# Keeping scaled attention tiles in PSUM and issuing a projection piece between a step's scores and its transposes

## The chip, the cores and the metric

The kernel runs on one core of one Trainium2 chip. The core's engines work side by side, each through its own queue in order: TensorE (PE, with PEld for its weight loads), VectorE (DVE), ScalarE (ACT), GpSimd (POOL) and SyncE (SP, which here only starts transfers). The metric is the device time of one execution in microseconds. The runs of the kernel before took 1247.38, 1249.82 and 1250.08 us; their median, 1249.82 us, is the time to compare with.

## The reference

A two-layer encoder trunk over 512 positions and 1024 channels, in fp32. Layer 0 is a state-space mixer and a gated MLP; layer 1 is a differential attention and a gated MLP. The change lies in the attention alone:

```python
qkv = h @ w_qkv                                   # 8 heads, each with 2 q and 2 k of 64, one v of 128
q = q * (64 ** -0.5)
s = einsum('bqhtd,bkhtd->bhtqk', qi, k) + bias    # t = 0, 1
p = softmax(s)
pd = p[:, :, 0] - lam * p[:, :, 1]
out = einsum('bhqk,bkhe->bqhe', pd, v)
out = rmsnorm(out, subln_g) * (1.0 - lambda_init)
return out @ w_o
```

## The kernel before

Every matrix product is made of three fp32r matmuls (`mm3`): a value is held as a high part `hi` and a low part `lo` = value - `hi`, and hi by hi, hi by lo and lo by hi are added up in one PSUM bank. So each tile that feeds a product is first written as its high part by ACT, then as its low part by DVE, which needs the value and the high part. Weights are split in the same way: ACT writes the high part (line 139), and in the attention POOL writes the low part (line 141).

The attention is a hand-written order of 32 steps, four 128-row query blocks `q` for each of eight heads `hd`. PSUM has eight banks, given out by tag: `sc` 3, `tr` 1, `pj` 2, `pv` 1, `aux` 1. A step `i` issues:

- `scores(i)`: four matmuls (lines 1207 and 1210) into two `sc` banks, then on DVE two fused add-and-maximum operations (line 1214) and the negated maxima (line 1217).
- `lower()`: the low parts of a q or k projection that was scaled a step earlier (line 1141, two operations).
- `transp(i - 2)`: four transposes (line 1242) of the finished probabilities of step i - 2, ACT's copy to the high part (1244) and DVE's low part (1245). In a late step (i = 6, 10, 14, ...) `pv` comes here instead, the twelve matmuls of a finished head with v, and the transposes follow it.
- `expo(i)` (ACT, 1222), `norm2(i - 1)` (DVE, 1232: writes the probabilities that the next step transposes).
- `flush()`, which runs what waits in the list `post`: the scaling of a finished projection (`evac`), and the low part of a head's output.
- `fl()`, twice (once from step 25 on): a piece of other work, in `fill`. Up to step 24 it is a quarter of a q or k projection of a later head: two blocks of `mm3`, six matmuls (lines 778 to 780) into a `pj` bank. From step 25 on it is an output projection of heads 0 to 3, `ofull`, also into a `pj` bank.
- in some steps the head's RMS norm: `sub1` (row sums, and Newton steps on POOL), `sub2` (broadcast), and at the start of the next step `sub3`.

`evac` scales a projection's bank into an SBUF tile `tq` (line 1133); ACT copies `tq` to the high parts (1137) and, a step later, `lower()` subtracts (1141). `sub3` does the same for a head's output: line 1270 from the `pv` bank into `tq`, 1274 and 1275 for the two parts. Both `tq` come from tag `sqt`, which has two buffers.

The first head's two projections run ahead of the loop, each flushed, and `lower()` follows; then `fl(6)` issues six pieces, the first of which opens head 1's q projection.

Of the kernel before, what the change touches and what calls it, by code (L numbers as in the profile page):

```python
# [9 lines left out]
F32 = mybir.dt.float32  # L10
# [27 lines left out]
def trunk(ctx, tc, xs, xt, sp, bx, cx, sv, vec, lamv, biasw, wglu, wup, wdn, wv, wqk, wo, out):  # L38
# [3 lines left out]
    def pool(name, bufs, side=None, space=None):  # L42
        kw = dict(name=name, bufs=bufs, reuse_waits="tile")
        if side:
            kw["side"] = side
        if space:
            kw["space"] = space
        return tc.alloc_tile_pool(**kw)
# [7 lines left out]
    def arena(dt, shape, name):  # L56
        return ap_.tile(shape, dt, tag="A", name=name)
# [553 lines left out]
    def intra(bk):  # L611
        yp = ps2.tile([128, 4, 8, 16], F32, tag="yp", name="yp", bufs=6)
        yb[bk] = yp
        for pl in range(4):
            for e in range(2):
                gi = (bk * 4 + pl) * 2 + e
                PE.matmul(yp[64 * e:64 * e + 64, pl], lhsT=u[:, gi], rhs=TT[:, :, gi], start=(pl == 0), stop=False,
                          skip_group_check=True)
# [5 lines left out]
    def out_half(bk, half, dr):  # L624

        yp = yb[bk]
        j0 = 32 * half
        for pl in range(4):
            pr = bk * 4 + pl
            for e in range(2):  # L630
                gl = (pr % 8) * 2 + e
                r0 = 64 * e + j0
                PE.matmul(yp[r0:r0 + 32, pl], lhsT=IZ[:, j0:j0 + 32, dr, e, pr], rhs=W[pr // 8][:, dr, gl],
                          start=False, stop=True, skip_group_check=True, tile_position=(0, r0))
# [21 lines left out]
    for at_s, kind, bk in EV:  # L656
        f = {"w": wchunk, "i": lambda bk=bk: intra(bk), "y": lambda bk=bk: S.copy(ys[:, bk - NB], yb.pop(bk)), "f": lambda bk=bk: out_half(bk, 0, 0),
             "b": lambda bk=bk: out_half(bk, 1, 1)}[kind]
# [112 lines left out]
    wk = pool("wk", 1, "left")  # L771
# [5 lines left out]
    def mm3(ps, wh, wl, xh, xl, first, last):  # L777
        PE.matmul(ps, lhsT=wh, rhs=xh, start=first, stop=False)  # L778
        PE.matmul(ps, lhsT=wh, rhs=xl, start=False, stop=False)  # L779
        PE.matmul(ps, lhsT=wl, rhs=xh, start=False, stop=last)  # L780
# [75 lines left out]
    for un in range(4):  # L856
# [3 lines left out]
        for ml in range(2):  # L860
# [4 lines left out]
            ps = psd[0].tile([128, 512], F32, tag="mm", name="ps", bufs=6)  # L865
# [206 lines left out]
    def bank(tag, name):  # L1072
        return psd[0].tile([128, 512], F32, tag=tag, name=name, bufs={"sc": 3, "tr": 1, "pj": 2, "pv": 1, "aux": 1}[tag])
# [29 lines left out]
    post = []  # L1103
# [5 lines left out]
    def lower():  # L1109
        for f in lows:  # L1110
            f()
        lows.clear()

    def flush():
        for f in post:
            f()
        post[:] = hold
        hold.clear()

    def proj(hd, which):  # L1120

        st = {}

        def evac(ps):
            if which == 0:  # L1130
                qk[hd] = at.tile([128, 5, 512], F32R, tag="qk", name="qkt", bufs=2)
            tq = wk.tile([128, 512], F32, tag="sqt", name="tq", bufs=2)
            V.scalar_tensor_tensor(tq, ps, 0.125 if which == 0 else 1.0, rbt, op0=ALU.mult, op1=ALU.mult)
            t = qk[hd]
            rows = (slice(0, 64), slice(64, 128))
            for c in range(2):
                S.activation(t[rows[c], 2 * which + c], tq[rows[c]], AF.Copy)

            def low():
                for c in range(2):  # L1140
                    V.tensor_tensor(t[rows[1 - c], c] if which == 0 else t[rows[c], 4], tq[rows[c]],  # L1141
                                    t[rows[c], 2 * which + c].bitcast(F32), op=ALU.subtract)

            lows.append(low)
            if which == 1:
                for c in range(2):
                    G.dma_start(out=t[rows[1 - c], 2 + c], in_=t[rows[c], 2 + c])

        def part(k0):
            def f():  # L1150
                if k0 == 0:
                    st["w"] = ws.start()
                    st["ps"] = bank("pj", "pj")
                if k0 % 4 == 0:
                    ws.split(k0 // 4, eng=G)
                wh, wl = st["w"]
                for k in range(k0, k0 + 2):
                    mm3(st["ps"], wh[:, k * 128:k * 128 + 128], wl[:, k * 128:k * 128 + 128], xhi[:, k], xlo[:, k],
                        k == 0, k == 7)
                if k0 == 6:  # L1160
                    post.append(lambda: evac(st["ps"]))
            return f
        return [part(k0) for k0 in (0, 2, 4, 6)]
# [33 lines left out]
    def load_bias(hd):  # L1197
        biases[hd] = at.tile([128, 896], F32, tag="bias", name="bias", bufs=2)
        SY.dma_start(out=biases[hd], in_=biasw[hd])

    def scores(i):
        hd, q = divmod(i, 4)
        t = qk[hd]
        mx = mxs[i] = at.tile([128, 8], F32, tag="mx", name="mx", bufs=4)
        pss = [bank("sc", "sc") for _ in range(2)]
        for c in range(2):
            PE.matmul(pss[c], lhsT=t[:, c, 128 * q:128 * q + 128], rhs=t[:, 2 + c], start=True, stop=False)
        for c in range(2):
            r = slice(64 * c, 64 * c + 64)
            PE.matmul(pss[c], lhsT=t[r, c, 128 * q:128 * q + 128], rhs=t[r, 4], start=False, stop=True)  # L1210
        sc[i] = []
        for c in range(2):
            s = at.tile([128, 512], F32, tag=f"s{c}", name="s", bufs=3 - c)
            V.tensor_tensor_reduce(s, pss[c], biases[hd][:, 384 - 128 * q:896 - 128 * q], op0=ALU.add, op1=ALU.max,
                                   scale=1.0, scalar=-3.0e38, accum_out=mx[:, c:c + 1])
            sc[i].append(s)
        V.tensor_scalar(mx[:, 2:4], mx[:, 0:2], -1.0, None, op0=ALU.mult)

    def expo(i):
        mx = mxs[i]  # L1220
        for c in range(2):
            S.activation(sc[i][c], sc[i][c], AF.Exp, bias=mx[:, 2 + c:3 + c], accum_out=mx[:, 4 + c:5 + c])

    def norm1(i):
        mx = mxs[i]
        V.reciprocal(mx[:, 6:8], mx[:, 4:6])
        V.tensor_tensor(mx[:, 7:8], mx[:, 7:8], nlam, op=ALU.mult)
        S.activation(sc[i][1], sc[i][1], AF.Copy, scale=mx[:, 7:8])
# [8 lines left out]
    def transp(i):  # L1237
        pd = pds.pop(i)
        q = i % 4
        ps = bank("tr", "ptp").rearrange("p (k t) -> p k t", t=128)  # L1240
        for kt in range(4):
            PE.transpose(ps[:, kt], pd[:, 128 * kt:128 * kt + 128], ident)
        hi, lo = ptt[:, :, 0, 128 * q:128 * q + 128], ptt[:, :, 1, 128 * q:128 * q + 128]
        S.activation(hi, ps, AF.Copy)
        return lambda: V.tensor_tensor(lo, ps, hi.bitcast(F32), op=ALU.subtract)
# [16 lines left out]
    def sub2(hd):  # L1262
        ps, _, rt = pvs.pop(hd)
        rb = rstd_bcast(rt, 128)
        pvs[hd] = (ps, rb)

    def sub3(hd):
        ps, rb = pvs.pop(hd)
        tq = wk.tile([128, 512], F32, tag="sqt", name="tq", bufs=2)
        V.scalar_tensor_tensor(tq, ps, gsub, rb, op0=ALU.mult, op1=ALU.mult)  # L1270
        if hd % 4 == 0:
            ot[hd // 4] = arena(F32R, [128, 4, 2, 512], f"o{hd}")
        o = ot[hd // 4]
        S.activation(o[:, hd % 4, 0], tq, AF.Copy)
        post.insert(0, lambda: V.tensor_tensor(o[:, hd % 4, 1], tq, o[:, hd % 4, 0].bitcast(F32), op=ALU.subtract))
# [14 lines left out]
    def fl(n=1):  # L1290
        for _ in range(n):
            if fill:
                fill.pop()()

    fl(6)
    for i in range(32):
        hd, q = divmod(i, 4)
        if q == 0 and 0 < hd < 7:
            load_bias(hd + 1)
        if i >= 9 and q == 1:  # L1300
            sub3((i - 9) // 4)
        if i >= 1:
            norm1(i - 1)
        scores(i)
        lower()
        late = i >= 6 and i % 4 == 2
        lo = transp(i - 2) if i >= 2 and not late else None
        if late:
            pv((i - 6) // 4)
        expo(i)  # L1310
        if lo:
            lo()
        if i >= 1:
            norm2(i - 1)
        if late:
            transp(i - 2)()
        flush()
        if i < 25:
            fl()
        if i >= 8 and q == 0:  # L1320
            sub2((i - 8) // 4)
        fl()
        if late:
            sub1((i - 6) // 4)
# [163 lines left out]
```

## Time and profile before

| what | value |
|---|---|
| median of the runs | 1249.82 us (1247.38 to 1250.08) |
| profiled execution, its own time | 1246.88 us |
| its span, first to last instruction | 1245.1 us |
| PE busy over the span | 1175.8 us, 94% |
| DVE busy | 824.9 us, 66% |
| ACT busy | 581.6 us, 47% |
| POOL busy | 253.5 us, 20% |
| mean granted TensorE clock | 0.982 |

The profiled execution is about 3 us below the median. Its span leaves out 1.8 us of its own time. Step 0 of the attention begins near 651 us and step 31 near 823 us of the span.

### The profile page before, as it was taken

The page shows a single profiled execution, that of the slowest core. Times are in us where ns is not written, and L with a number is a line of the kernel's source. Part 1 is how long each engine was busy: PE and PEld are TensorE (multiplying, and loading weights), DVE is VectorE, ACT ScalarE, POOL GpSimd, SP SyncE. Part 2 cuts the span into 40 slices and gives each one's busy share as a digit, 9 for nine tenths or more (in the row PEclk, how much of TensorE's full clock was granted, in tenths as well). Part 3 has the DMA queues.
Part 4 walks back from the last instruction along what each step waited for, and adds up shares of the span by engine and source line. Part 5 has one row for each costly group of instructions (what it writes and reads, how often), then busy time and mean ns, then how long its engine had stood idle before and what let it go on. Part 6 is the DMA issues. An engine that isn't in the chain of part 4 may idle for free.

```text
span 1245.1 us, 16497 instructions
## 1 busy us (share of the span) xinstructions
PE 1175.8 (94%) x6338; PEld 930.0 (75%) x6338; DVE 824.9 (66%) x1650; ACT 581.6 (47%) x1001; POOL 253.5 (20%) x271
## 2 busy tenths in 40 slices
PE   3875899999999999999998999999999999999996
PEld 1663588888878888878876777678888878888786
DVE  7989866676752467754339899976767643566634
ACT  6864655444431244333337777755444422344431
POOL 3899434000000000011033444523000000000011
PEclk8997999999999999999999999999999999999998
DMA  5005322122233222132332323221222233122222
GB/s 219 2 2 136 135 75 102 68 102 84 75 117 115 68 102 101 58 106 77 99 123 82 90 74 87 88 73 67 98 71 99 81 117 125 68 92 78 93 94 68
DMA packets 23391, 112.32 MB, mean 90 GB/s; under 512 B 2704, under 2 KB 5392, under 8 KB 16144
## 3 DMA queue, kind: packets, MB, share of 16 engines
q1 hardware_dynamic: 21472, 108.64, 25.7%
q0 software_dynamic: 1280, 2.10, 0.9%
q8 instruction: 50, 0.82, 0.3%
q10 hardware_dynamic: 560, 0.52, 0.1%
q14 instruction: 29, 0.24, 0.1%
HBM read 102.86 MB, written 2.10 MB: 84 GB/s over the span
## 4 chain that ended last, share of the span: by engine, by line
PE 83%; DVE 14%; ACT 2%; issue 1%; DMA 0%; SPq 0%; DVEq 0%; ACTq 0%
PE ps L779 20%; PE ps L778 20%; PE ps L780 20%; DVE scn L678 2%; PE pj L778 2%; PE pj L780 2%; PE pj L779 2%; DVE St L683 1%; PE vps L1088 1%; DVE qkt L1141 1%; PE vps L1090 1%; PE vps L1089 1%; DVE acc L681 1%; PE po L779 1%; PE po L780 1%; PE po L778 1%
## 5 line engine op out<-in xcount | busy, mean ns | idle before, releaser
L778 PE MATMUL ps<-xhi,hi 128*128 128x512 f32 x672 | 266.9, 397 | 0.0
L779 PE MATMUL ps<-xlo,hi 128*128 128x512 f32 x672 | 265.7, 395 | 0.0
L780 PE MATMUL ps<-xhi,lo 128*128 128x512 f32 x672 | 264.1, 393 | 0.0
L139 ACT ACTIVATE hi<-raw 128x1024 fp32r<-128x1024 f32 (+2 forms) x216 | 184.1, 874 | 113.5 <-PE ps L779 85.8
L141 DVE TENSOR_TENSOR lo<-raw,hi 128x1024 fp32r<-128x1024 f32 (+3 forms) x178 | 188.3, 1077 | 43.5 <-ACT hi L139 41.8
L903 DVE TENSOR_TENSOR tpb<-ps,rb 128x512 f32<-128x512 f32 x88 | 60.8, 693 | 149.7 <-PE ps L780 144.5
L905 ACT ACTIVATE acc<-tpb,vect 128x512 f32<-128x512 f32 x88 | 71.6, 816 | 168.2 <-DVE tpb L903 168.2
L780 PEld LDWEIGHTS ps<-xhi,lo 128*128 128x128 f32 x672 | 126.1, 188 | 31.5
L778 PEld LDWEIGHTS ps<-xhi,hi 128*128 128x128 f32 x672 | 126.1, 188 | 30.6
L779 PEld LDWEIGHTS ps<-xlo,hi 128*128 128x128 f32 x672 | 126.2, 188 | 29.5
L779 PE MATMUL ps<-act,hi 128*128 128x512 f32 (+1 forms) x374 | 144.1, 385 | 0.2
L778 PE MATMUL ps<-act,hi 128*128 128x512 f32 (+1 forms) x374 | 142.8, 382 | 0.0
L780 PE MATMUL ps<-act,lo 128*128 128x512 f32 (+1 forms) x374 | 142.1, 380 | 0.0
L803 POOL COPY ssum<-sqt 128x512 f32<-128x512 f32 x4 | 2.5, 627 | 658.5 <-ACT sqt L800 658.5
L981 DVE TENSOR_TENSOR h<-ps,h 128x512 f32<-128x512 f32 x30 | 20.7, 690 | 107.5 <-PE ps L780 107.5
L141 POOL TENSOR_TENSOR lo<-raw,hi 128x512 fp32r<-128x512 f32 (+1 forms) x38 | 61.0, 1611 | 114.2 <-ACT hi L139 114.1
L778 PEld LDWEIGHTS ps<-act,hi 128*128 128x128 f32 x374 | 70.3, 188 | 15.8
L780 PEld LDWEIGHTS ps<-act,lo 128*128 128x128 f32 x374 | 70.2, 188 | 15.9 <-DVE lo L141 1.4
L779 PEld LDWEIGHTS ps<-act,hi 128*128 128x128 f32 x374 | 70.2, 188 | 15.3 <-DVE act L922 1.1
L911 DVE SCALAR_TENSOR_TENSOR acc<-tpb,vect,acc 128x512 f32<-128x512 f32 x88 | 66.2, 752 | 3.1
L910 DVE SCALAR_TENSOR_TENSOR acc<-tpb,vect,acc 128x512 f32<-128x512 f32 x88 | 65.5, 744 | 0.6 <-ACT acc L905 0.6
L921 ACT ACTIVATE act<-acc 128x512 fp32r<-128x512 f32 x44 | 27.9, 634 | 66.2 <-DVE acc L920 66.2
(260 smaller groups left out, 2035.7 us busy)
## 6 DMA issues: line engine op xcount, KB each, us to landing
raw<-wup SPq DMA_DIRECT2D x44, 1024.0 KB, 4.8
raw<-wdn SPq DMA_DIRECT2D x32, 704.0 KB, 4.0
raw<-wqk SPq DMA_DIRECT2D x16, 512.0 KB, 3.5
raw<-wglu SPq DMA_DIRECT2D x4, 1024.0 KB, 4.9
raw<-wv SPq DMA_DIRECT2D x8, 512.0 KB, 3.5
raw<-wo SPq DMA_DIRECT2D x4, 1024.0 KB, 4.8
bias<-biasw SPq DMA_DIRECT2D x8, 448.0 KB, 4.1
cxt<-cx SPq DMA_DIRECT2D x1, 2064.0 KB, 15.8
```

The lines of the kernel that those rows point to most:

```text
L139: S.activation(hi[:, h0:h1], self.raw[i][:, h0:h1], AF.Copy)
L141: eng.tensor_tensor(lo[:, h0:h1], self.raw[i][:, h0:h1], hi[:, h0:h1].bitcast(F32), op=ALU.subtract)
L678: V.tensor_tensor(prd[dr], cur[:, dr].unsqueeze(1).to_broadcast([128, 2, 2, 32]), cft[dr], op=ALU.mult)
L778: PE.matmul(ps, lhsT=wh, rhs=xh, start=first, stop=False)
L779: PE.matmul(ps, lhsT=wh, rhs=xl, start=False, stop=False)
L780: PE.matmul(ps, lhsT=wl, rhs=xh, start=False, stop=last)
L903: V.tensor_tensor(tb[:, 1:513], ps, state["rb"], op=ALU.mult)
L905: S.activation(acc, tb[:, 1:513], AF.Identity, bias=cb, scale=cw[1])
L910: V.scalar_tensor_tensor(acc, tb[:, 0:512], cw[0], acc, op0=ALU.mult, op1=ALU.add)
L911: V.scalar_tensor_tensor(acc, tb[:, 2:514], cw[2], acc, op0=ALU.mult, op1=ALU.add)
L921: S.activation(hi, a0, AF.Copy)
L981: V.tensor_tensor(h[:, m], ps, h[:, m], op=ALU.add)
```

## The change

Two things. First, `evac` and `sub3` no longer scale into an SBUF tile: they write the scaled values back to the PSUM bank that they read, and ACT's copy to the high part and DVE's low part read that bank. Second, in a step up to 24 the first of the two pieces is issued right behind `lower()`, ahead of the transposes or `pv`; the list `post` is taken before it and run where `flush()` stood.

```diff
@@ proj(): evac
             if which == 0:
                 qk[hd] = at.tile([128, 5, 512], F32R, tag="qk", name="qkt", bufs=2)
-            tq = wk.tile([128, 512], F32, tag="sqt", name="tq", bufs=2)
+
+            tq = ps
             V.scalar_tensor_tensor(tq, ps, 0.125 if which == 0 else 1.0, rbt, op0=ALU.mult, op1=ALU.mult)
@@ sub3()
         ps, rb = pvs.pop(hd)
-        tq = wk.tile([128, 512], F32, tag="sqt", name="tq", bufs=2)
+        tq = ps
         V.scalar_tensor_tensor(tq, ps, gsub, rb, op0=ALU.mult, op1=ALU.mult)
@@ the loop over steps
         scores(i)
         lower()
         late = i >= 6 and i % 4 == 2
+        todo = post[:]
+        post.clear()
+        if i < 25:
+            fl()
         lo = transp(i - 2) if i >= 2 and not late else None
         if late:
             pv((i - 6) // 4)
...
             norm2(i - 1)
         if late:
             transp(i - 2)()
-        flush()
-        if i < 25:
-            fl()
+        for f in todo:
+            f()
         if i >= 8 and q == 0:
             sub2((i - 8) // 4)
         fl()
```

## Rows read from the trace of the kernel before

**Rows 1.** Windows, steps 7 to 22: PE, PEld, DVE, ACT, POOL us; clock; DMA

```profile
688.00:776.00 88.00, 87.08 (x434) 66.28 (x434) 80.61 (x177) 68.82 (x144) 38.58 (x77) 1.00 0.31 87
```

**Rows 2.** Waits view of the attention: us in total, times, longest

```profile
PE ptp L1242 <- DVE s L1232: 4.7, 6, 2.9
```

**Rows 3.** Timeline, transposes that waited: start, us, engine, line, [idle before <- releaser]

```profile
660.99 0.66 PE L1242 MATMUL ptp<-ident,s 128*128 128x128 f32 x4 [0.82 <-DVE s L1232]
667.05 0.63 PE L1242 MATMUL ptp<-ident,s 128*128 128x128 f32 x4 [1.69 <-DVE mx L1226]
677.02 0.63 PE L1242 MATMUL ptp<-ident,s 128*128 128x128 f32 x4 [1.35 <-DVE mx L1226]
699.01 0.63 PE L1242 MATMUL ptp<-ident,s 128*128 128x128 f32 x4 [0.24 <-DVE s L1232]
...
789.66 0.52 PE L1242 MATMUL ptp<-ident,s 128*128 128x128 f32 x3 [2.92 <-DVE s L1232]
```

**Rows 4.** Views of tiles and lines, whole attention: ns min/median/max

```profile
L1141 DVE TENSOR_TENSOR qkt<-tq,qkt x32: 676/686/3161, 643.9 to 797.4; 64x512 fp32r<-64x512 f32 x32
...
L1245 DVE TENSOR_TENSOR pt<-ptp,pt x32: 678/691/693, 665.6 to 835.2; 128x512 fp32r<-128x512 f32 x32
...
L1217 DVE TENSOR_SCALAR mx<-mx x32: 168/170/1244, 653.8 to 825.1; 128x2 f32<-128x2 f32 x32
```

**Rows 5.** Timeline, a weight split on POOL and DVE's operation beside it

```profile
698.24 1.76 POOL L141 TENSOR_TENSOR lo<-raw,hi 128x512 fp32r<-128x512 f32 x1 [2.18 <-ACT hi L139]
...
698.78 0.74 DVE L1270 SCALAR_TENSOR_TENSOR tq<-pvp,gsub,rb 128x512 f32<-128x512 f32 x1
```

**Rows 6.** Timeline, start of head 1's q projection

```profile
642.92 0.39 PE L778 MATMUL pj<-xhi,hi 128*128 128x512 f32 x1
...
643.92 0.68 DVE L1141 TENSOR_TENSOR qkt<-tq,qkt 64x512 fp32r<-64x512 f32 x1
```

**Rows 7.** Timeline, step 1 from its first piece to the next scores

```profile
656.21 0.50 PE L778 MATMUL pj<-xhi,hi 128*128 128x512 f32 x1
656.31 0.69 DVE L1214 CUSTOM_DVE_ANT_0 s<-sc,bias 128x512 f32<-128x512 f32 x1 [0.43 <-PE sc L1210]
...
657.65 1.06 DVE L1217 TENSOR_SCALAR mx<-mx 128x2 f32<-128x2 f32 x1
...
658.75 1.40 DVE L1141 TENSOR_TENSOR qkt<-tq,qkt 64x512 fp32r<-64x512 f32 x2
...
659.12 0.62 PE L1207 MATMUL sc<-qkt 128*128 128x512 f32 x2
```

**Rows 8.** Timeline, the late step 10 (first two) and steps 11 and 12

```profile
702.62 0.68 DVE L1275 TENSOR_TENSOR o<-tq,o 128x512 fp32r<-128x512 f32 x1
...
703.28 0.50 PE L778 MATMUL pvp<-pt,v 128*128 128x512 f32 x1
...
713.37 0.74 DVE L1232 SCALAR_TENSOR_TENSOR s<-s,mx 128x512 f32<-128x512 f32 x1
...
714.54 0.20 POOL L162 TENSOR_TENSOR t<-t 128x4 f32<-128x4 f32 x1
...
715.62 0.69 DVE L1214 CUSTOM_DVE_ANT_0 s<-sc,bias 128x512 f32<-128x512 f32 x1 [0.64 <-PE sc L1210]
...
716.77 1.28 POOL L141 TENSOR_TENSOR lo<-raw,hi 128x512 fp32r<-128x512 f32 x1 [2.04 <-ACT hi L139]
```

**Rows 9.** Timeline, steps 25 and 26

```profile
786.62 2.34 POOL L141 TENSOR_TENSOR lo<-raw,hi 128x1024 fp32r<-128x1024 f32 x1 [0.53 <-ACT hi L139]
...
787.26 2.25 DVE L1232 SCALAR_TENSOR_TENSOR s<-s,mx 128x512 f32<-128x512 f32 x1
...
796.71 3.51 DVE L1141 TENSOR_TENSOR qkt<-tq,qkt 64x512 fp32r<-64x512 f32 x2
...
797.13 0.48 PE L778 MATMUL po<-o,hi 128*128 128x512 f32 x1
```

## The prediction

> **What bounds the kernel now.** I read four views in this order. The windows view of steps 7 to 22 comes first [rows 1]: PE is busy for 87.08 of 88 us at full granted clock, and DVE for 80.61. So the attention is PE's, with a DVE that has some 1.8 us left in the 22 us of a head: what is taken from PE's waits is a gain, and what makes DVE late can soon become a wait of PE. Then the view of waits, for what PE lacks [rows 2]: almost all of its idle time stands in front of the transposes (line 1242), which wait for `norm2` of the step before (1232). Then the timeline at each of these waits [rows 3]: three early ones of 0.82, 1.69 and 1.35 us (sum 3.86), four of about 0.23, one in each head (sum 0.92; one is shown), and one of 2.92 in step 25. Together that is 7.70 us, and it is all that the move can win. Last, for the PSUM half of the change, the timeline around the moments at which PE opens a bank that DVE has just read: steps 0, 1, 10, 26 and 30.
>
> **The change, part by part.**
>
> *Operations.* No instruction is added or removed. Sixteen operations of line 1133 and eight of 1270 write PSUM instead of SBUF, and 32 low parts (1141) and eight (1275) read PSUM. The nearest rows are two low parts of 512 columns: from SBUF 686 ns, from PSUM 691 [rows 4]. I take 0 for the price of a PSUM operand; the bound below is 0 too, and the one above 0.05 us, by which 1270 with its 0.74 [rows 5] stands above 691 ns, for each of eight operations in a head: 0.4 us where DVE sets the pace. [...]
>
> *What PSUM costs is the bank.* Before, a `pj` bank was free when 1133 had read it; now it is free when 1141 has, one step's `lower()` later. A `pv` bank was free after 1270, now after 1275. I go through each place where PE opens such a bank.
>
> (a) Ahead of the loop. Head 1's q projection takes the bank of head 0's q, and starts at 642.92 [rows 6]. The two low parts of that bank run from 643.92, and two of them take 1.40 [rows 7], so they end at 645.32. PE has nothing else queued: **+2.4 us**. Nothing hides it, and no row makes it shorter.
>
> (b) Step 1. Its first piece opens head 2's q, in the bank of head 1's q, which is scaled in step 0 and lowered in step 1 behind the scores' own DVE work. Before, the piece started at 656.21. The two 1214 operations take from 656.31 to 657.65, 1217 a further 0.17 where nothing holds it [rows 4] (1.06 here), and the low parts 1.40 [rows 7]: 659.22. **+3.0 us**, with bounds of 2.8 (1217 hidden) and 3.9 (held again). From step 3 on a bank is lowered one whole step before it is opened, so this does not come back while projections run.
>
> (c) The early waits. Twelve matmuls of two pieces take 2.91 us, from 656.21 to 659.12 [rows 7], so one piece covers 1.45 us. The waits of 0.82, 1.69 and 1.35 come when DVE is late against PE; after (b) PE is itself 3 us later and has 1.45 of cover on top. All go: **-3.86 us** [rows 3].
>
> (d) Four heads, steps 7 to 22. The four small waits, 0.23 each, go under the piece. But the piece also delays the transposes by 1.45, and with them ACT's copy (1244), behind which `expo` and DVE's 1245 and 1232 are queued; and the weight split (139) that the piece issues is now ahead of that copy, so POOL's part of it (141) starts ahead of 1232. In step 11 POOL is first busy with the Newton steps until 714.74, and its split would then run to 716.02 (1.28 long). 1232 reads two SBUF tiles, and such an operation waits for POOL to end: in step 25 it began 0.64 us into POOL's work and took 2.25 instead of 0.74 [rows 9]. So 1232 of step 11 starts near 716.0 instead of 713.37, 2.65 later; DVE had 0.64 to spare before step 12's scores, so it goes into step 12 some 2.0 us late [rows 8]. If that lag lasts to 1275 in step 13, it reaches `pv`: before, 1275 ended at 703.30 and `pv` began at 703.28, so there was no margin, and the piece in front gives 1.45. A wait of 0.55, less the 0.23 won: +0.3 a head, **+1.2 us**. Bounds for a head: -0.23 if DVE catches up, and +1.2 if POOL blocks one more small operation on the way, by 0.89 (1217 with 1.06 instead of 0.17) [rows 4, 7].
>
> (e) Step 25 (2.92). From this step on no piece stands between scores and transposes. What made the wait is 1232 behind a wide POOL split of 2.34 us [rows 9]. In the new order ACT issues that split just ahead of the copy, and 1245 (0.69) and then 1232 follow the copy, so POOL's 2.34 still covers the start of 1232. I take **0** won; the bound below is all 2.92.
>
> (f) Steps 26 and 30. In step 26 the output projection opens the bank of the last k projection at 797.13, whose low parts start at 796.71 and take 1.40 now that they are not held: 798.11, **+1.0 us**; before they took 3.51, but no one waited. In step 30 `pv` needs the bank that 1275 gives up, with the margin of step 10, none [rows 8], and now without a piece to cover it: between 0 and the 1.0 of step 26, **+0.5**.
>
> Queues: the piece's weight transfer moves forward on SP, past no other entry of that queue, and is not read before the next projection two steps on. On POOL the split moves ahead of the two copies of k (1147), which then start up to 1.28 us later; the scores that read them come three steps on. Both cost nothing as long as a step lasts some 5.5 us, a quarter of the 22 us of a head.
>
> Sum: 2.4 + 3.0 - 3.86 + 1.2 + 0 + 1.0 + 0.5 = **+4.2 us**. On the profiled execution's own 1246.88 (span 1245.1 and 1.8 around it) that is 1251.1; this execution lies 2.9 below the median, so against 1249.82 I forecast **1254.0 us**.
>
> **The rivals.**
>
> *POOL lets go of DVE, and the lag never forms (not slower).* Line 1141 was at times held for up to 3.16 us [rows 4], and with one operand in PSUM it should not be: 1270, which reads PSUM too, ran its usual 0.74 right beside POOL [rows 5]. The room so won would go to 1232: then (d) is -0.92, (e) is -2.92 and (f) 0, with (a), (b) and (c) as above: -2.3, so 1247.5 us. For it: 80.61 us of DVE include such holds. Against: the operations on the way to the transposes, 1232 and 1217, still read SBUF alone. It decides once DVE enters step 12 less than 1.4 us late. [...]
>
> *DVE becomes the bound.* Each of the four heads pays the 1.2 of (d)'s upper bound: 4.2 + 3.6 = +7.8, 1257.6 us. For it: 1.8 us of room in a head. Against: part of DVE's work is lighter without holds.
>
> *The banks don't hold PE.* Were a bank released at 1133 still, (a), (b) and the 1.0 of (f) fall away: 4.2 - 6.4 = -2.2, and less if the lag is smaller too, to -7: 1243 to 1247.6. Against: line 1141 reads the bank, so the bank is in use until then.
>
> **How the numbers follow.** Forecast 0.52, POOL lets go 0.27, DVE the bound 0.15, no hold 0.06. The likeliest gives 1254.0, its own range 1251.5 to 1256.5. The bounds added up reach from -2.3 (nothing in (d) to (f) but what is won) to +9.2 (0.9, 3.6 and 0.5 more in (b), (d) and (f)); all of one sign at once is unlikely, so I cut them at -1.8 and, just short of the second rival's +7.8, at +7.7, which leaves some 2 in 10 out: 1248.0 to 1257.5. About 0.2%, 2.5 us, is what a measurement of this kernel tells from no change. Slower: 0.47 of the forecast and 0.15, 0.62. Faster: 0.05 of the second case and 0.04 of the last, 0.09. Same: the rest, 0.29.
>
> **What would show it.** In the profile after: a PE gap of about 2.4 us before head 1's q projection and one of 3 us in step 1, both released by line 1141 (a, b); no wait before the transposes of steps 2, 3 and 5 (c); in each late step a wait of `pv` for 1275 of about half a microsecond (d); 1232 long beside POOL and a wait of 2 to 3 us in step 25 (e); line 1141 near 0.69 us in every row. The forecast is wrong if `pv` never waits and step 25's wait is gone (the first rival), or if the gaps at (a) and (b) are missing.

## The result, and the profile after

The changed kernel took 1257.40 us (median of six runs, 1255.54 to 1258.78) against 1249.31 us of the kernel before beside it (six runs, 1247.38 to 1250.08): 1.0065 of it, with a 95% interval of 1.0052 to 1.0078, so some 8 us slower. The profiled execution spans 1253.8 us where that of before spans 1245.1: 8.7 us more, and these 8.7 are what I account for. All line numbers of the changed kernel that matter here are one higher than before: 1142 are the low parts of q and k, 1211 the second score matmuls, 1233 `norm2`, 1243 the transposes, 1271 and 1276 the output's scaling and low part.

First the waits view of the changed kernel, attention and what follows it (engine, tile and line, what it waited for: us in total, times, longest):

```profile
PE pj L778 <- ACT s L1223: 3.1, 1, 3.1
PE ptp L1243 <- DVE s L1233: 2.7, 1, 2.7
PE pj L778 <- DVE qkt L1142: 2.3, 1, 2.3
PE ps L945 <- DVE h L1182: 1.7, 1, 1.7
PE pvp L778 <- DVE o L1276: 0.9, 1, 0.9
```

Of the six waits of transposes for `norm2` in [rows 2] one is left, in step 25; four others have come, each at the opening of a PSUM bank. The timeline shows the first two (start, us, engine, line, idle before and its releaser):

```profile
642.42 0.40 PE L780 MATMUL pj<-xhi,lo 128*128 128x512 f32 x1
...
643.59 2.81 DVE L1142 TENSOR_TENSOR qkt<-pj,qkt 64x512 fp32r<-64x512 f32 x4
...
645.12 0.47 PE L778 MATMUL pj<-xhi,hi 128*128 128x512 f32 x1 [2.30 <-DVE qkt L1142]
...
658.05 0.50 PE L1211 MATMUL sc<-qkt 64*128 64x512 f32 x2
...
660.13 1.39 DVE L1142 TENSOR_TENSOR qkt<-pj,qkt 64x512 fp32r<-64x512 f32 x2
...
661.67 0.76 PE L778 MATMUL pj<-xhi,hi 128*128 128x512 f32 x1 [3.11 <-ACT s L1223]
...
662.23 0.63 PE L779 MATMUL pj<-xlo,hi 128*128 128x512 f32 x1
662.66 0.63 PE L780 MATMUL pj<-xhi,lo 128*128 128x512 f32 x1
...
667.63 0.50 PE L1211 MATMUL sc<-qkt 64*128 64x512 f32 x2
```

At the start, PE stands still until the first two of four low parts have read the bank, at 645.0 (half of 2.81 behind 643.59). In step 1 the profile names ACT's line 1223, which has no part in that bank; the low parts end at 661.52, 0.15 us ahead of the matmul, and it is they who give the bank back. The reader should also see what follows: the matmuls start 0.43 us apart, where the same ones start 0.23 apart in [rows 7] (twelve in 2.91 us). The windows view says why. Its columns are the stretch and its length, PE, PEld, DVE, ACT and POOL busy (x instructions), the granted clock, the DMA share and GB/s:

```profile
656.00:660.00 4.00, 2.56 (x12) 1.55 (x10) 2.48 (x10) 3.70 (x8) 0.00 (x0) 1.00 0.25 101
660.00:664.00 4.00, 2.33 (x6) 1.88 (x7) 3.15 (x7) 2.57 (x7) 1.31 (x2) 0.55 0.01 2
664.00:668.00 4.00, 4.00 (x12) 2.77 (x10) 0.00 (x0) 1.52 (x3) 2.29 (x3) 0.59 0.42 74
668.00:672.00 4.00, 4.00 (x22) 2.99 (x20) 3.75 (x9) 1.80 (x4) 0.00 (x0) 1.00 0.38 123
...
693.30:781.30 88.00, 87.95 (x432) 65.69 (x430) 74.23 (x175) 67.48 (x144) 34.98 (x75) 1.00 0.29 83
...
793.00:794.50 1.50, 0.26 (x2) 0.29 (x3) 1.50 (x2) 0.61 (x3) 0.55 (x1) 0.68 0.00 0
794.50:796.00 1.50, 1.50 (x7) 1.31 (x6) 1.47 (x6) 1.20 (x3) 0.00 (x0) 0.50 0.88 246
796.00:797.50 1.50, 1.50 (x6) 1.22 (x5) 1.38 (x5) 1.50 (x5) 0.00 (x0) 0.68 1.03 437
797.50:799.00 1.50, 1.50 (x9) 1.18 (x7) 1.50 (x4) 0.50 (x2) 0.00 (x0) 1.00 0.04 16
```

Behind the long gap in step 1 the granted clock is 0.55 and 0.59 in the rows of 660 and 664 (0.50 from 661 to 667 alone), and behind step 25's wait it falls to 0.50 again, in the row of 794.50. The row of 693.30 answers to [rows 1]: in the same 88 us PE is now busy for 87.95 instead of 87.08, DVE for 74.23 instead of 80.61. So DVE is far from becoming the bound. A higher busy share is not less time, though: from the second score matmuls of step 7 to those of step 23, the sixteen steps take 88.40 us now (692.92 to 781.32) and took 87.96 before (688.82 to 776.78). Most of the time is lost at the two ends of the attention.

The other three waits, on the timeline: step 25 (the answer to [rows 3] and [rows 9]), step 30, and the first feed-forward matmuls:

```profile
791.19 2.35 POOL L141 TENSOR_TENSOR lo<-raw,hi 128x1024 fp32r<-128x1024 f32 x1 [4.16 <-ACT hi L139]
...
792.38 1.72 DVE L1233 SCALAR_TENSOR_TENSOR s<-s,mx 128x512 f32<-128x512 f32 x1
...
794.24 1.08 PE L1243 MATMUL ptp<-ident,s 128*128 128x128 f32 x4 [2.70 <-DVE s L1233]
...
821.58 0.68 DVE L1276 TENSOR_TENSOR o<-pvp,o 128x512 fp32r<-128x512 f32 x1
...
822.41 0.47 PE L778 MATMUL pvp<-pt,v 128*128 128x512 f32 x1 [0.89 <-DVE o L1276]
...
866.10 0.39 PE L946 MATMUL ps<-xlo,hi 128*128 128x512 f32 x1
...
867.37 0.68 DVE L1182 TENSOR_TENSOR h<-po,h 128x512 f32<-128x512 f32 x1
...
868.19 0.47 PE L945 MATMUL ps<-xhi,hi 128*128 128x512 f32 x1 [1.70 <-DVE h L1182]
```

And two lines of the views of tiles (ns min/median/max), 1142 of the changed kernel for 1141 of [rows 4], and 1271 for the 1270 of [rows 5]:

```profile
L1142 DVE TENSOR_TENSOR qkt<-pj,qkt x32: 675/689/696, 643.6 to 802.0; 64x512 fp32r<-64x512 f32 x32
...
L1271 DVE SCALAR_TENSOR_TENSOR pvp<-pvp,gsub,rb x8: 748/757/759, 703.7 to 853.4; 128x512 f32<-128x512 f32 x8
```

A low part with one operand in PSUM takes 3 ns more in the median (689 for 686), and is not held once in its 32 times here: its longest falls from 3161 to 696 ns.

Taking the start of each step's second score matmuls (1210, then 1211) in both profiles gives where the 8.7 us arose:

| term of the sum | predicted | measured |
|---|---|---|
| (a) up to step 0 | +2.4 | +2.27 |
| (b) step 1 | +3.0 | +5.69 |
| (c) steps 2 to 5 | -3.86 | -3.87 |
| (d) steps 6 to 24 | +1.2 | +0.71 |
| (e) step 25 | 0 | +1.02 |
| (f) step 26 | +1.0 | 0.0 |
| (f) step 30 | +0.5 | +0.92 |
| behind step 31 | - | +1.96 |
| sum | +4.2 | +8.70 |

So my theory for the experiments: banks that are given back by the low parts hold PE where I said, but two of the PE gaps are followed by some microseconds of TensorE at about half its clock (0.50 from 661 to 667 and from 794.5 to 796), and a bank is handed to the next stage one h-add later. The rivals: VectorE is slower on PSUM operands, or the moved pieces delay ACT and POOL.

### The profile page after: what moved, and what is told of

Its sections match the earlier page's. It is cut to its first block, busy times and chain, and to the rows that moved or that the text cites. A ratio compares the mean times of both kernels' runs of the same rounds, so it can differ in the third digit from the quotient of the medians.

```text
span 1253.8 us, 16499 instructions
## 1 busy us (share of the span) xinstructions
PE 1181.7 (94%) x6338; PEld 931.2 (74%) x6338; DVE 810.6 (65%) x1650; ACT 580.0 (46%) x1001; POOL 248.7 (20%) x271
## 4 chain that ended last, share of the span: by engine, by line
PE 83%; DVE 4%; ACT 2%; POOL 1%; issue 1%; DMA 0%; DVEq 0%; ACTq 0%; POOLq 0%
PE ps L779 20%; PE ps L778 20%; PE ps L780 20%; PE pj L778 3%; PE pj L780 2%; PE pj L779 2%; PE vps L1088 1%; PE vps L1090 1%; PE vps L1089 1%; PE sc L1208 1%; PE ptp L1243 1%; PE sc L1211 1%; PE pvp L778 1%; PE st L811 1%; PE po L779 1%; PE po L778 1%
## 5 line engine op out<-in xcount | busy, mean ns | idle before, releaser
L141 POOL TENSOR_TENSOR lo<-raw,hi 128x512 fp32r<-128x512 f32 (+1 forms) x38 | 58.0, 1533 | 128.9 <-ACT hi L139 128.9
L778 PE MATMUL pj<-xhi,hi 128*128 128x512 f32 x128 | 56.3, 439 | 5.4 <-ACT s L1223 3.1
```

The lines of the kernel that those rows point to most:

```text
L141: eng.tensor_tensor(lo[:, h0:h1], self.raw[i][:, h0:h1], hi[:, h0:h1].bitcast(F32), op=ALU.subtract)
```

## The experiments

Each time is a median, each ratio is to the kernel before that ran beside it; the span is that of its profile.

| kernel | us | ratio, 95% interval | span |
|---|---|---|---|
| e1, order alone | 1244.58 | 0.9959 (0.9947 to 0.9971) | 1241.8 |
| e2, PSUM alone | 1256.03 | 1.0048 (1.0034 to 1.0061) | 1254.7 |
| e3, bank named early | 1257.49 | 1.0062 (1.0050 to 1.0074) | 1255.7 |
| e4, PE kept busy | 1254.00 | 1.0036 (1.0024 to 1.0048) | 1252.8 |
| e5, banks exchanged | 1254.05 | 1.0048 (1.0036 to 1.0061) | 1252.3 |
| e6, and early low parts | 1245.02 | 0.9977 (0.9966 to 0.9988) | 1242.7 |
| e7, output alone in PSUM | 1247.70 | 0.9997 (0.9988 to 1.0006) | 1244.3 |
| e8, order, step 25 too | 1246.29 | 0.9986 (0.9977 to 0.9995) | 1243.8 |
| e9, order alone again | 1244.82 | 0.9977 (0.9965 to 0.9988) | 1242.4 |
| e10, e6 with output in SBUF | 1243.63 | 0.9967 (0.9955 to 0.9980) | 1240.7 |

**The two halves, each alone.** e1 undoes the PSUM half, in both places:

```diff
-            tq = ps
+            tq = wk.tile([128, 512], F32, tag="sqt", name="tq", bufs=2)
```

> The pieces are issued as in the changed kernel, but q, k and output are scaled into an SBUF tile as in the kernel before. Theory (banks and clock: the loss comes from PSUM banks that are held until the low parts, and from the lower granted clock after the two long PE waits): the gaps of 2.3 us ahead of head 1's q projection and of 3 us in step 1 are not there, nor the low clock behind the latter; the three early transposes' waits stay away (-3.9 us); step 25 keeps a wait of 2.7 us and perhaps its lower clock after it (+1). Together about 2 to 4 us faster than before, 1245.5 to 1247.5 us. Rival (order: the pieces ahead of the transposes make the ACT copies and POOL's part later, and that is what costs): the time stays above before, by 2 us or more. Rival (PSUM operands make DVE slower): about -4, too; it is told from the theory by the other kernels.

e2 undoes the order:

```diff
-        todo = post[:]
-        post.clear()
-        if i < 25:
-            fl()
...
-        for f in todo:
-            f()
+        flush()
+        if i < 25:
+            fl()
```

> q, k and output stay in PSUM for their low parts, but the pieces are issued where the kernel before issues them, behind the transposes. Theory (banks and clock): +2.3 us ahead of head 1's q projection, a PE gap of 3 us or less in step 1, the three early waits of transposes stay in part: +3 to +6 us, 1252.5 to 1255.5; if the granted clock falls behind the gap in step 1 the upper end. Rival (PSUM operands make DVE slower): all of the changed kernel's +8 and the early waits on top, +8 to +12 us. Rival (order): near 0 beyond the 2.3 us at the start.

The order alone gains 4.6 us, the PSUM half alone loses 6.9 (1256.03 and 1244.58 against 1249.13). So the rival "order" falls: what the moved pieces delay costs less than the order wins. The waits view of e1 over the attention:

```profile
PE ptp L1243 <- DVE mx L1227: 0.4, 1, 0.4
...
PE ptp L1243 <- DVE s L1233: 2.8, 1, 2.8
```

and e2: two waits that stand ahead of a bank (665.43 and 800.71) and, between them, what leads up to the transposes of step 25 (timeline):

```profile
665.43 0.76 PE L778 MATMUL pj<-xhi,hi 128*128 128x512 f32 x1 [4.01 <-ACT s L1222]
...
791.28 2.40 POOL L141 TENSOR_TENSOR lo<-raw,hi 128x1024 fp32r<-128x1024 f32 x1 [2.38 <-ACT hi L139]
...
791.33 1.39 DVE L1141 TENSOR_TENSOR qkt<-pj,qkt 64x512 fp32r<-64x512 f32 x2
...
793.34 0.88 DVE L1232 SCALAR_TENSOR_TENSOR s<-s,mx 128x512 f32<-128x512 f32 x1
794.87 2.40 POOL L141 TENSOR_TENSOR lo<-raw,hi 128x1024 fp32r<-128x1024 f32 x1 [1.19 <-ACT hi L139]
...
800.71 0.47 PE L778 MATMUL pvp<-pt,v 128*128 128x512 f32 x1 [1.50 <-DVE o L1275]
```

The kernel before has this in its step 24, for the 791.33 of e2:

```profile
783.14 3.50 DVE L1141 TENSOR_TENSOR qkt<-tq,qkt 64x512 fp32r<-64x512 f32 x2
```

Three things are to be seen here. In e2 the transposes hardly wait in steps 2, 3 and 5 either (0.34 us, in step 5), though no piece stands ahead of them: it is nearly enough that PE comes late. Each half wins most of these waits (steps 2 to 5 are 2.9 us shorter than before in e1, 3.5 in e2), but together they win them only once. Second, beside a POOL split of 2.40 us the two low parts, with one input in PSUM, take 1.39 us; in the kernel before two of them, with both inputs in SBUF, take 3.50 us beside a split of 2.92 (783.17 to 786.09). Third, in the old order the second wide split starts at 794.87, behind `norm2`, and step 25's wait is gone: PSUM alone wins the 2.9 us of [rows 3] there, and the new order takes it back, because POOL's split then lies beside 1233 (791.19 above). But e2 gives more than half of it back one step later: step 26 takes 9.54 us instead of 7.96, because `pv` waits 1.50 us for the bank of the output (800.71). My expectation for e2 had neither that wait, nor the late bank behind step 31 (1.7 us here too), nor a low clock behind the gap at the start, which its profile shows (0.79 and 0.78 from 644 to 652).

**The clock.** e4 puts matmuls into the two gaps, in step 1 into the `aux` bank and in step 25 into an `sc` bank; nobody reads what they write:

```diff
         if i < 25:
             fl()
+        if i in (1, 25):
+            dm = bank("aux" if i == 1 else "sc", "dm")
+            for n in range(12 if i == 1 else 10):
+                PE.matmul(dm, lhsT=xhi[:, 0, 0:128], rhs=xhi[:, 1], start=True, stop=True)
```

> The changed kernel with 12 matmuls of 512 columns in step 1 and 10 in step 25 added, into a PSUM bank of their own whose result nobody reads, placed where TensorE waits. Theory (clock): the waits themselves stay, but TensorE is busy in them, the granted clock stays at its full level behind them, and the following matmuls are 0.22 to 0.23 us apart instead of 0.43: 2.0 to 2.5 us less in step 1, about 1 us less in step 25, 1253.9 to 1254.4 us. Rival (what follows the waits is slow because DVE and ACT are late, not for the clock): no gain, or the cost of whatever part of the 22 matmuls (5 us) doesn't fit in the waits, 1257.4 to 1260.

3.4 us less than the changed kernel, with 22 matmuls more. Timeline of its step 1, and its windows there:

```profile
660.60 0.50 PE L1211 MATMUL sc<-qkt 64*128 64x512 f32 x2
661.03 3.01 PE L1313 MATMUL dm<-xhi 128*128 128x512 f32 x12
664.21 0.47 PE L778 MATMUL pj<-xhi,hi 128*128 128x512 f32 x1 [0.17 <-ACT s L1223]
664.51 0.40 PE L779 MATMUL pj<-xlo,hi 128*128 128x512 f32 x1
...
667.64 0.50 PE L1211 MATMUL sc<-qkt 64*128 64x512 f32 x2
```

```profile
660.00:664.00 4.00, 4.00 (x17) 2.55 (x15) 3.12 (x9) 3.94 (x9) 1.12 (x1) 1.00 0.01 2
664.00:668.00 4.00, 3.83 (x17) 2.74 (x16) 1.73 (x5) 2.55 (x6) 1.24 (x3) 1.00 0.11 22
```

Step 1 takes 7.04 us (660.60 to 667.64) instead of 9.58 (658.05 to 667.63). The bank is given back as late as before, but the clock stays at 1.00: 2.5 us of (b) is the clock, and 3.1, which is 7.04 less the 3.9 of a step before, the bank. Step 25 takes 7.10 instead of 8.28. The rival, late DVE and ACT work, would have left both as they were.

**The bank at the end.** e3 names block 5's bank ahead of block 4's:

```diff
     part(3, "tr")
+    pp[5] = bank("pj", "po")
     part(4, "pj", (0,))
```

> The changed kernel with one line more: the PSUM bank of the first block of the feed-forward part that comes after the attention's last normalisation is named ahead of the block before it, so that the two blocks exchange their banks. No work is added. Theory (banks): the PE gap of 2.1 us ahead of the first feed-forward matmul that opens its second bank goes, and the time falls by 1.7 to 2.1 us against the changed kernel, to about 1255.4 us. Rival (the gap is the later h-add itself, and would be met at the next bank): no change, 1257.4.

Nothing changed (1257.49 us, the 2.1 us gap still there). Taken alone that speaks for the rival; but the traces do not number the banks, so it is not shown that the one line exchanged them at all. e5 exchanges them by their tags:

```diff
-    part(3, "tr")
+    part(3, "pj")
...
-    part(5, "pj")
+    part(5, "tr")
```

> The changed kernel, with the PSUM banks of two blocks of the last output projection exchanged (block 3 takes one of the two projection banks, block 5 the transposes' bank), so that the bank that the first feed-forward matmuls open second was last read by block 4's h-add instead of block 5's. Theory (the bank that is handed over is released one h-add too late): the PE gap of 2.1 us at the first feed-forward matmuls goes, and the time is 1.7 to 2.1 us less than the changed kernel's, about 1255.4 us. Rival (the gap is made by something else that the changed kernel delays, such as the split of the weights): the gap stays, 1257.4 us. Third: block 5 now waits for the transposes' bank or block 4 for a projection bank, and the gap moves ahead by some blocks: 1257 us, with a new wait of PE in the projection.

1.0048 against 1.0065: 2.1 us less, though the two intervals overlap. The profile decides it: from the second score matmuls of step 31 to the end e5 takes 421.94 us, as the kernel before does (421.93), and the changed kernel 423.89. The matmuls of its feed-forward part follow each other without the gap (866.53 and 866.76 here for 866.10 and 868.19 above):

```profile
866.29 0.40 PE L945 MATMUL ps<-xhi,hi 128*128 128x512 f32 x1
866.53 0.39 PE L946 MATMUL ps<-xlo,hi 128*128 128x512 f32 x1
866.76 0.39 PE L945 MATMUL ps<-xhi,hi 128*128 128x512 f32 x1
```

**The low parts of the first two heads, earlier.** e6 is e5 with

```diff
     for f in proj(0, 0) + proj(0, 1):
         f()
+        lower()
         flush()
...
     fl(6)
+    flush()
+    lower()
```

> The kernel of the run before it in this list, with the low parts of the first two heads issued earlier: after each piece of head 0 in the preface, and once after head 1's q ahead of the loop. Nothing is added. Theory (banks and clock): the 2.3 us ahead of head 1's q projection and the 3.1 us in step 1 go, and with the latter the low granted clock behind it (2.5 us); in exchange the early transposes of steps 2, 3 and 5 may wait again for what their 3.86 us exceed the piece's cover of 1.45 us each, at most 0.5 us. So 7 us less than the run before it, 1247.5 to 1249.5 us. Rival (slower DVE operations on PSUM operands, whose sum stays the same): the two gaps go but come back as waits in the steps behind, no more than 2.3 us gained, 1253 us or more.

9 us less than e5, and faster than the kernel before. In its profile both gaps are gone, PE is busy for all 20.00 us from 640 to 660 at full clock, and the transposes of steps 2 to 5 do not wait. The 9 us are more than I expected, because step 25 has no low clock in this profile (1.00 from 776 to 802 and 7.02 us, where e5 has 0.58 from 794 to 798 and 8.27 us). The rival of slow PSUM operands, which allowed 2.3 us, is out.

**Which of the two PSUM edits.** e7 keeps only the output in PSUM (the edit of e1 in `evac` alone):

> The changed kernel, but q and k are scaled into an SBUF tile as before; only the scaled output of the subtraction step stays in PSUM. Theory (banks): of the PSUM half only the waits of the bank of the attention output are left: 0.25 us in each of the four heads of steps 7 to 22 and 0.9 in step 30, 1.9 us more than the kernel with the order alone (1244.6), so 1246 to 1247 us; the gaps at the start and in step 1 and their low clock are not there, and the bank handed over at the end is the one of the kernel before. Rival (PSUM operands are slow on DVE, each operation alike): a third of the changed kernel's difference to the order alone, since 8 of 24 scalings and 8 of 40 low parts are left: 1248.9 us.

e10 is e6 with the output, and that alone, scaled into SBUF:

> The changed kernel with early low parts for the first two heads and the exchanged banks, and with the output scaled into SBUF again, so that only q and k stay in PSUM. Theory (banks): against the same kernel with the output in PSUM as well, the waits for the bank of the attention output go: 0.25 us in each of four heads and 0.9 in step 30, 1.9 us less, 0.9962 of the kernel before, 1243 to 1244.5 us; level with the order alone. Rival (the output's bank is not what costs): 0.9977 as before, and the step 30 still 8.9 us long.

In e7 the waits for the bank of the output are there (step 30 8.90 us long for 7.98 in e1, the late steps of the four heads 0.16 to 0.18 longer each), and so is a low clock in step 25 (0.88 in the mean from 776 to 790), 8.62 us long for 7.10; that clock's 1.5 us is more than the 0.7 by which it came out above what I expected. Its time alone would not rule out the rival's 1248.9; the same operations in the profiles before and after do: the eight scalings take 757 ns in the median in PSUM where they took 744 into SBUF (1271 and 1270), and the eight low parts 680 for 684 (1276 and 1275), which is under 0.1 us in all. e10 loses these waits again (step 30 7.98 us) and has one wait left in the attention. Its time is 1.4 us below e6's where 1.9 were expected, with ratios whose intervals overlap. Its waits view:

```profile
PE ptp L1243 <- DVE s L1233: 2.7, 1, 2.7
```

**Step 25.** e8 is e1 with step 25's piece issued ahead of its transposes:

```diff
-        if i < 25:
+        if i < 26:
             fl()
...
-        fl()
+        if i != 25:
+            fl()
```

> The kernel with the order alone (scaling into SBUF), with step 25's only piece, the first block of the output projection of the first half, issued ahead of that step's transposes too. Theory (PE's order decides what the wait for the last step's normalisation costs): that piece is 12 matmuls, 2.8 us, and takes the place of the 2.8 us wait in step 25; steps 26 on as before: 1244.6 - 2.8 = 1241.8 us, 1241 to 1243. Rival (the transposes are late anyway and delay ACT's copy, expo and the next steps' normalisation): the wait comes back in step 26 or 27, 1244 us or more.

The rival was right. The 2.8 us wait goes, and comes back as several: 

```profile
787.80 0.50 PE L1208 MATMUL sc<-qkt 128*128 128x512 f32 x1 [0.58 <-DVE mx L1215]
789.63 0.50 PE L778 MATMUL pvp<-pt,v 128*128 128x512 f32 x1 [0.90 <-ACT pt L1245]
790.36 0.50 PE L779 MATMUL pvp<-pt,v 128*128 128x512 f32 x1 [0.23 <-DVE pt L1246]
798.54 0.66 PE L1243 MATMUL ptp<-ident,s 128*128 128x128 f32 x4 [0.37 <-DVE pt L1246]
```

By step 28 it stands level with e1 (802.41 and 802.42), and the first feed-forward matmuls then show the gap of the late bank (1.7 us). Yet e8 keeps no scaled tile in PSUM: the order of the pieces alone can hand a bank over late.

**Second profiles** of e1, e7 and the changed kernel:

> The kernel with the order alone (scaling into SBUF) a second time, as the one to beat on this chip. 0.41% less than the kernel before was measured: 1243.5 to 1245.5 us. Its step 25 with the 2.8 us wait took 7.10 us in its first profile, with the granted clock at 1.00 behind the wait. If the fall of the clock behind such a wait differs from execution to execution, this profile may show 8 us or more there.

> A second profile of the kernel with the output in PSUM alone. In the first, step 25 took 8.62 us, with a low granted clock behind its 2.8 us wait. If the fall of the clock differs from execution to execution of one program, step 25 may take 7.1 us here at 1.00; if it belongs to the program (where its matmuls lie), it takes 8.6 again.

> A second profile of the changed kernel itself. In the first, the 2.3 us wait ahead of head 1's q was not followed by a lower clock, the wait in step 1 was, and step 25 took 8.28 us. If it differs from execution to execution, some of these three change: up to 2.2 us more at the start, 2.5 less in step 1, 1.2 less or 1.5 more in step 25. If it belongs to the program, all three are as they were.

All three repeat their first profiles: step 25 took 7.10 us again in e9 and 8.66 in e11, and the changed kernel had 9.67 us in step 1, 8.31 in step 25 and no low clock at its start (1.00 from 640 to 660). But up to step 25 e3 is the changed kernel, and there it took 9.76; and e4, the same program up to step 1, had the clock at 0.75 and 0.83 from 644 to 652, behind the 2.3 us gap after which four profiles of that same start kept 1.00. So it is not the program alone. In time, e9 gains 3.2 us (0.9977) where e1 gained 4.6 (0.9959); the two intervals just overlap.

## Why the prediction was right, and where its sum was not

The direction was right, and so was the mechanism of the gaps, but 4.2 us were forecast and 8.1 came. That the range still held the time, by 0.1 us, is luck: some 5.7 us came from what the sum did not have (2.5 and 1.2 of low clock, 1.96 behind step 31), and 1.5 that it had did not come (step 26, and part of (d)).

- **(a), (b), (c)**: right. The waits are where they were put: 2.27 us, 3.1 us (as e4 separates it) and 3.87 us won; e6 removes the first two. For (c) I gave two reasons, PE's own delay and the piece's cover; e2, with the delay alone, wins 3.5 of it, e1, with the cover alone, 2.9. In e6 and e10 PE is not late, and all 3.9 are won: the cover and the early low parts do it there.
- **The step that failed** is the one behind (b) and (e): a gap of PE was counted as its length, as if what follows ran at full clock. In the kernel before it does, behind 2.92 us too (1.00 from 788 to 793). Here step 1 paid 2.5 us more, and step 25 1.2 more, shown by e4.
- **(e)** itself, the wait, was right and for the reason given: 1233 lies beside POOL's split in the new order (1.72 us), and e2 shows that in the old order it would have gone.
- **(f), step 26**: wrong, 0 instead of 1.0, and with it the premise that the projection opens the bank of those low parts. The changed kernel itself can't show it: its low parts ran from 801.27 to 802.66, and the projection opened at 802.95. They came 1.95 us behind the step's score matmuls (799.32), instead of 3.21 before (796.71 behind 793.50), because the low clock of step 25 (0.50) had held PE up; where the clock stayed at 1.00 (e4, e6, e10) it is 3.2 again. There the projection starts while the low parts still run. e4:

```profile
801.40 1.38 DVE L1142 TENSOR_TENSOR qkt<-pj,qkt 64x512 fp32r<-64x512 f32 x2
...
801.94 0.48 PE L778 MATMUL po<-o,hi 128*128 128x512 f32 x1
```

Had it opened their bank it would have waited, as at (a) and (b); so it takes the other of the two `pj` banks. If the two alternate from there, the last block holds the other bank too, which would make the late bank behind step 31; this link is argued, not shown. Step 30: right in kind, 0.92 for 0.5.
- **(d)**: too much, 0.71 for 1.2, and of the 0.71 only 0.44 lie in steps 7 to 22. `pv` waits only 0.2 of the 0.55 in each late step: in step 10 it starts 0.42 us behind the matmul ahead of it (708.92 and 708.50), where 0.23 is usual. 1233 of step 11 took 1.35 us beside POOL, but it began 3.82 us behind the step's second score matmuls (718.84 and 715.02) instead of 2.56 (713.37 and 710.81), so 1.3 late and not 2.65.
- **Behind step 31** the sum had nothing; 1.96 us, shown by e5 to be the bank's; the prediction looked for openings of a bank no further than step 30.

"DVE becomes the bound" gave nearly the measured time, 1257.6, and is wrong: DVE has 6.4 us more room in 88 than before. "POOL lets go" was right for 1141, never held now, and by its own sign too: DVE enters step 12 1.1 us late (1.66 behind the second score matmuls, 721.01 and 719.35, instead of 0.53). It was wrong for the late steps, which still lose 0.26 us each, and for the wait of step 25. "The banks don't hold PE" is refuted by (a) and (b).

What decides whether the clock falls behind a gap stays open: gaps of 2.7 to 2.9 us in step 25 kept 1.00 in five profiles (before, e1, e9, e6, e10) and lost it in six (the changed kernel twice, 0.50 from 794.5 to 796 and 0.57 from 794 to 798; e3, 0.50 from 794.5 to 800.5; e5, 0.58 from 794 to 798; e7, 0.88 from 776 to 790; e11, 0.74 from 790 to 794).

Below the kernel before, clear of their intervals, are the order alone (1244.58 and 1244.82), e10 (1243.63), e6 (1245.02) and e8 (1246.29). The intervals of the order alone and e10 overlap, so that the PSUM half, even where its banks hold no one, has not been shown to gain in time. In the profiles steps 2 to 5 are 0.9 us shorter in e10 than in e1, but e10's low parts were also moved forward.

## What to carry to other kernels

When a tile is kept in PSUM longer, list every place where the matrix engine opens a bank of that tag, the next stage's first ones too, and compare each with the end of the new last reader; the steady loop may pay little (0.44 us in sixteen steps here) while the start and the end pay much. Check in the profile which bank an opening really gets: step 26 took another one than I had assumed. Count a gap of TensorE at its length and, as the upper bound, add what the next microseconds lose if the clock falls behind it; here it fell to 0.50, and that was nothing to 2.7 us (step 25 took 7.10 us in e1 at 1.00 and 9.76 in e3 at 0.50). Two halves of a change that each remove the same wait don't add up.

## What the hardware showed that I had not expected

A low clock behind a gap of only 2.3 us at the start (from 644 to 652, 0.79 and 0.78 in e2, 0.75 and 0.83 in e4), and none behind 2.92 us in the kernel before (1.00 from 788 to 793); at a clock of 0.50 twelve matmuls took 5.25 us (661.67 to 666.92) where 2.91 is usual. Step 1 had 0.55 and 0.59 behind a wait of 3.11 us, and step 25 fell to 0.50 behind one of 2.70. So the length of the wait alone does not tell the falls from the rest in these runs.
